# FFN down-projection: high and low parts of f 64 bytes apart, their products in turn; other activations on multiples of 256

## The chip, the cores and the metric

The kernel runs on one core of a Trainium2 chip. The metric is the device time of one execution in microseconds (us). A traced execution has a span (first to last instruction of the program) besides its time.

## The reference, cut to what matters

Two blocks for a sequence of 256 tokens of width 1024, in float32. The second half of the first block is a convolutional feed-forward network (FFN); the products in question are its last line, and every other product with a 1024-wide weight matrix shares the tiles that are moved:

```
def _conv_ffn(h, w_up, conv_w, conv_b, w_down):
    a, g = jnp.split(h @ w_up, 2, axis=-1)          # 2 x 2816 columns
    a = lax.conv_general_dilated(a, conv_w[:, None, :], window_strides=(1,), padding=[(CONV_W - 1, 0)], ...) + conv_b
    return (jax.nn.gelu(a) * g) @ w_down            # 2816 x 1024
...
    h = _rmsnorm(x, norm_g[l, 2]) * (1.0 + sc2) + sh2
    y = _conv_ffn(h, w_up[l], conv_w[l], conv_b[l], w_down[l])
    x = x + g2 * _rmsnorm(y, norm_g[l, 3])
```

Before it stands a mixer (projections of h, three small attentions, gates, an output projection); behind it a second block: a gated linear attention layer and a layer of dilated window attention, each with projections in and out and a layer norm.

## The kernel before, in words

Every float32 operand of a large product is split into a high part (rounded to float32r, "hi") and a low part (the rest, "lo"), and each product is three matmuls: lo times hi, hi times lo, hi times hi. `mm3` issues them in this order, its first operand being the stationary one (loaded by LDWEIGHTS, the profile's PEld), its second the moving one (streamed by MATMUL). In the profile's names the moving operand stands first: `acc<-whi,flo` streams whi past flo.

Weights come through `Stream`: an SP DMA fetches a chunk of 2048 columns into `raw`, ScalarE casts each half to `whi` (L158), VectorE subtracts to get `wlo` (L159). There are three raw buffers and six buffers each of whi and wlo, that is three chunks of two parts; a cast waits until TensorE is through with the buffer it writes. The chunks follow one order written out at L282 to L322; `get` casts two chunks ahead.

Two forms of product use them. `wpair` and `wstat` hold weights stationary and stream 256 tokens of an activation (output columns in partitions): the first projections, the gates, the FFN's up-projection, and the query and key projections. For these keys (`STILL`) wlo lies 64 bytes behind a multiple of 128, whi on one. `tokmm` holds 128 tokens of an activation stationary and streams 512 columns of a weight: the output projections, values, and FFN down. There wlo lies on a multiple of 128.

Activations that feed these products stand in pairs made by `big8`: tiles of 8192 bytes and 128 more in each partition, in a tag of two buffers 8320 bytes apart, so one buffer lies on a multiple of 256 and the other 128 bytes past one. hhi and h2hi (L401, L916) take the first buffer and hlo and h2lo the second; mhi and x2hi (L792, L967) the second, mlo and x2lo the first. `past` moves a tile by so many floats: h2lo by 64 bytes, x3hi by 32 and x3lo by 96. The pairs yhi/ylo (L626) and ohi/olo (L1110) are tiles of their own, all on multiples of 256.

The FFN (L952 to L962) runs over 22 row tiles f of 128 columns of the inner width. `ffn_up(f)` is one `wpair` of 48 products, then the convolution, Gelu, the multiplication and the split into `fhi` (L947, ScalarE) and `flo` (L948, VectorE), each 128 x 256 in a tag of six buffers of 1024 bytes. After every second tile one chunk of w_down is multiplied with the two tiles before: for each tile u, both blocks b of 128 tokens, both halves c of the 1024 output columns, the three products of `mm3` in a row; 24 products of 512 columns for a chunk. Two chunks are left for the end, where all four tiles are done for b=0 and then for b=1, there bank by bank. The sums lie in four PSUM banks (`acc`) for the whole loop. Behind it `rms_residual` (ORD2) and `transposes` make x2 and its transposed split x2hi/x2lo.

x2 lies in a pool `res` that stays open to the end of the kernel; pools p3 (gated linear attention) and p4 (window attention) lie behind it.

Of the kernel before, what the change touches and what calls it, by code (L numbers as in the profile page):

```python
# [9 lines left out]
F32R = mybir.dt.float32r  # L10
# [8 lines left out]
S = 256  # L19
D = 1024  # L20
KK = 8
# [177 lines left out]
def wsl(w, a, b):  # L199

    part, parts = w
    i = a // part
    assert b <= (i + 1) * part
    return tuple(t[:, a - i * part:b - i * part] for t in parts[i])
# [26 lines left out]
def hybrid_blocks(ctx, tc, A, out, dbg=None):  # L231
# [3 lines left out]
    cn = Lines(ctx.enter_context(tc.tile_pool(name="cn", bufs=1)), sm)  # L235
# [3 lines left out]
    def open_pool(name):  # L239
        st = ExitStack()  # L240
        p = st.enter_context(tc.tile_pool(name=name, bufs=1))
        return Lines(p, st.enter_context(tc.tile_pool(name=name + "s", bufs=1))), st.close
# [4 lines left out]
    def acc_t():  # L247

        return [ps.tile([128, 512], F32, tag="acc", name="acc", bufs=4) for _ in range(2)]

    def mm_t():
        return ps.tile([128, 512], F32, tag="mm", name="mm", bufs=2)
# [8 lines left out]
    def mm(o, l, r, start, stop, share=False):  # L261
        return pe.matmul(o, l, r, start=start, stop=stop, skip_group_check=share)  # L262
# [8 lines left out]
    def mm3(o, l, r, start, stop, share=False):  # L271
        mm(o, l[1], r[0], start, False, share)
        mm(o, l[0], r[1], False, False, share)
        return mm(o, l[0], r[0], False, stop, share)

    def sl(pair, *ix):
        return tuple(t[ix] for t in pair)
# [74 lines left out]
    def col(name, i):  # L352
        o = COLS[name] + i
        return cols[:, o:o + 1]
# [40 lines left out]
            mm(pr[:, 256 + b:257 + b], ssq[:, b * 128:(b + 1) * 128], ones[:, 0:1], h == 0 and b == 0, h == 3, True)  # L395

    def big8(dt, name, past=0):
        t = cn.tile([128, KK * S + 32], dt, name=name, tag="big8r", bufs=2)
        return t[:, past:past + KK * S].rearrange("p (k s) -> p k s", k=KK)

    hT = (big8(F32R, "hhi"), big8(F32R, "hlo"))  # L401
# [6 lines left out]
    def gemv(raw):  # L408

        g = p0.tile([128, 2], F32, name="gv", tag="gv", bufs=3)  # L410
        for u in range(2):
            t = p0.tile([128, D], F32, name="gj", tag="gj", bufs=1)
            ins = dve.scalar_tensor_tensor(t, raw[:, u * D:(u + 1) * D], 1.0, crow, op0=OP.mult, op1=OP.mult, accum_out=g[:, u:u + 1])
        return g, ins
# [68 lines left out]
    with tc.high_priority(400):  # L483
        ga, ins = gemv(raw)
# [8 lines left out]
    for j in range(KK):  # L493
        cur = h32
        ws.behind = at
        raw, w = ws.get(("in1", j), 1 if j + 1 < KK else None)
# [14 lines left out]
    wk = p1  # L511
# [10 lines left out]
    def wpair(key, a, fresh=False):  # L522


        w = ws.get(key)
        p = mm_t()
        if fresh:
            for n in range(2):
                o = p[:, n * 256:(n + 1) * 256]
                W = [wsl(w, n * 1024 + k * 128, n * 1024 + (k + 1) * 128) for k in range(KK)]  # L530
                for k, l in enumerate(W):
                    mm(o, l[1], a[0][:, k, :], k == 0, False)
                    mm(o, l[0], a[0][:, k, :], False, False)
                for k, l in enumerate(W):
                    mm(o, l[0], a[1][:, k, :], False, k == KK - 1)
            return p
        for n in range(2):
            wstat(p[:, n * 256:(n + 1) * 256], w, n * 1024, a)
        return p
# [199 lines left out]
    def gates(i):  # L739
        p = wpair(("zg", i), hT)  # L740
        for u in range(2):
            n, br = (i, u) if i < 8 else (2 * (i - 8) + u, 2)
            act.activation(th[:, n, min(br, 1), :], p[:, u * 256:(u + 1) * 256], AF.Tanh, scale=0.5,
                           bias=bgh[:, br * 8 + n:br * 8 + n + 1])
        next(att, None)
# [30 lines left out]
    for i in range(2):  # L776
        w = ws.get(("br", i))
        for u in range(4):
            n = 4 * i + u
# [7 lines left out]
        if i:  # L787
            w2 = ws.get(("br", 2))
            branch2(0)
            branch2(1)  # L790
        gates(9 + 2 * i)
    mT = (big8(F32R, "mhi"), big8(F32R, "mlo"))  # L792
    for i in range(4):
        if i > 1:
            branch2(i)
        merged(i)

    def tokmm(accs, work, width, first, last, bs=(0, 1), banks=(False, False)):


        for b in bs:
            steps = [(v, c) for v in enumerate(work) for c in range(0, width, 512)]
            if banks[b]:
                steps.sort(key=lambda v: v[1])
            for (i, (aT, k, w, base)), c in steps:
                l = sl(aT, slice(None), k, slice(b * 128, (b + 1) * 128))
                e = min(c + 512, width)
                ins = mm3(accs[b][c // 512][:, 0:e - c], l, wsl(w, base + c, base + e), first and i == 0, last and i == len(work) - 1)
        return ins.ins

    def tokproj(accs, keys, aT, width, tail=1, look=None, i=0):

        n = len(keys)
        while i < n:
            m = tail if i == n - tail else 1
            work = []
            for j in range(i, i + m):
                w = ws.get(keys[j], look if i == n - tail else None)
                work += [(aT, 2 * j + u, w, u * width) for u in range(2)]
            for part in ([work] if m > 1 else [work[0:1], work[1:2]]):  # L820
                ins = tokmm(accs, part, width, i == 0 and part is not work and part[0] is work[0] or (i == 0 and part is work),
                      i + m == n and part[-1] is work[-1], banks=(False, m > 1))
            i += m
        return ins
# [3 lines left out]
    last_mm = tokproj(y, [("out", i) for i in range(4)], mT, 1024, 2, 1)  # L828
# [73 lines left out]

    close_p1()
    close_p1a()
    res, _ = open_pool("res")
    ctx.callback(_)
    p2, close_p2 = open_pool("p2")
    wk = p2
    xn = p2.tile([128, 2, D], F32, name="xn")
# [22 lines left out]
    y2 = [acc_t(), acc_t()]  # L932
    fact = {}

    def ffn_up(f):
        p = wpair(("up", f), h2, f == 0)
        u = wk.tile([128, S], F32, name="u", tag="u", bufs=2)
        cw = lambda i: col("cw", i * NF + f)
        act.activation(u, p[:, 0:S], AF.Identity, scale=cw(2), bias=col("cb", f))
        dve.scalar_tensor_tensor(u[:, 1:S], p[:, 0:S - 1], cw(1), u[:, 1:S], op0=OP.mult, op1=OP.add)  # L940
        dve.scalar_tensor_tensor(u[:, 2:S], p[:, 0:S - 2], cw(0), u[:, 2:S], op0=OP.mult, op1=OP.add)
        act.activation(u, u, AF.Gelu_apprx_tanh)
        a = wk.tile([128, S], F32, name="fa", tag="fa", bufs=2)
        dve.tensor_mul(a, u, p[:, S:2 * S])
        hi = wk.tile([128, 1, S], F32R, name="fhi", tag="fhi", bufs=6)
        lo = wk.tile([128, 1, S], F32R, name="flo", tag="flo", bufs=6)
        ins = act.activation(hi[:, 0, :], a, AF.Copy)  # L947
        ins2 = dve.tensor_sub(lo[:, 0, :], a, hi[:, 0, :].bitcast(F32))  # L948
        fact[f] = (hi, lo)
        return ins, ins2  # L950

    for f in range(NF):  # L952
        ins = ffn_up(f)
        if f % 2 == 0 and 0 < f <= NF - LASTF:
            w = ws.get(("dn", f // 2 - 1))
            for u in range(2):
                tokmm(y2, [(fact[f - 2 + u], 0, w, u * 1024)], 1024, f == 2 and u == 0, False)
    work = []
    for i in range((NF - LASTF) // 2, NF // 2):
        w = ws.get(("dn", i), 1)  # L960
        work += [(fact[2 * i + u], 0, w, u * 1024) for u in range(2)]
    last_mm = tokmm(y2, work, 1024, False, True, banks=(False, True))  # L962

    x2 = res.tile([128, 2, D], F32, name="x2")
    rms_residual(y2, x1, mod[3], x2, ORD2)
# [7 lines left out]
    wk = p3  # L973
# [5 lines left out]
    w = ws.get(("gla", 8))  # L979
# [107 lines left out]
    for i in range(4):  # L1087
        w = ws.get(("gvg", i))
# [8 lines left out]
    for i in range(2):  # L1097
        w = ws.get(("gvg", 4 + i))
# [6 lines left out]
    work = []  # L1105
    for i in range(2, 4):
        w = ws.get(("gvg", 4 + i), 1)
# [5 lines left out]
    def gated(b, u, last):  # L1113

        qa, qd = Queue(tc, act, last[0]), Queue(tc, dve, last[1])
        with tc.high_priority(BOOST):
            t = sg[:, b, half(u)]
            qa.activation(t, pv[b][u], AF.Tanh, scale=0.5)
            qd.scalar_tensor_tensor(t, t, 1.0, pv[b][u], op0=OP.add, op1=OP.mult)
            qd.tensor_mul(t, t, on[:, b, half(u)])  # L1120
        return qa.last, qd.last
# [15 lines left out]
    last = ws.last  # L1137
    for u in range(2):
        last = gated(0, u, last)
    for u in range(2):  # L1140
        last = transpose_half(sg, 0, u, oT, mm_t(), last)
# [3 lines left out]
    w = ws.get(("gout", 0), 0)  # L1145
    work = [(oT, u, w, u * 1024) for u in range(2)]
    for u in range(2):
        last = gated(1, u, last)
    for u in range(2):
        tokmm(y3, work[u:u + 1], 1024, u == 0, False, (0,))  # L1150
        last = transpose_half(sg, 1, u, oT, at_t(), last)
# [3 lines left out]
    last_mm = tokproj(y3, [("gout", i) for i in range(4)], oT, 1024, 2, 1, 1)  # L1155
# [58 lines left out]
            nc.scalar.dma_start(x3d[b], x3[:, b, :])  # L1214

    close_p3()
    p4, close_p4 = open_pool("p4")
    ctx.callback(close_p4)
    wk = p4
# [89 lines left out]
    for h in range(8):  # L1309
# [8 lines left out]
        if h == 2:  # L1318
# [3 lines left out]
            for a in range(4):  # L1322
                for b in range(4):
                    q = (a % 2) * 64 + b * 16
# [7 lines left out]
        if h in (2, 6):  # L1332
            w = ws.get(("sout", h // 4))
# [4 lines left out]
    w = ws.get(("sout", 2)), ws.get(("sout", 3))  # L1338
    tokmm(y4, [(sact[4], 0, w[0], 0)], 1024, False, False)
    work = [(sact[5], 0, w[0], 1024)]  # L1340
# [103 lines left out]
```

## Time and profile before

| | |
|---|---|
| three runs | 741.21, 735.28, 741.20 us; median 741.2 |
| profiled execution: time, span | 733.62 us, 731.6 us |
| mean granted clock of the span | 0.986 |
| TensorE matmul busy | 700.6 us (96% of the span) |
| weight loads busy | 636.4 us (87%) |
| VectorE, ScalarE, GpSimd busy | 547.1, 407.1, 20.2 us |
| SP queue of the weights | 139.05 MB, 52.1% of 16 engines' span |

Matmuls overlap: a product of 256 columns is shown with some 0.28 us, one of 512 columns with 0.39 us, but the next one starts after a fraction of that. What a product costs a full TensorE is the step from its start to the next start.

### The profile page before, as it was taken

The numbers are of one execution on the slowest core, as the hardware profiler recorded it, in microseconds if no ns is written. First come the engines' busy times: TensorE is split into PE (matmuls) and PEld (weight loads), VectorE is DVE, ScalarE is ACT, GpSimd is POOL, SyncE is SP. The second block draws the span as 40 slices with busy tenths as digits, with TensorE's granted clock in tenths as the row PEclk, the third lists the DMA queues.
The fourth block names the chain that finished last, engine by engine and source line by source line (L and its number), as shares of the span: only waits on it lengthen the run. The fifth ranks groups of instructions, "written<-read, shape, count | busy, mean of one in ns | idle before, by whom it ended". The sixth has DMA issues, their size and how long they took to land. (4 is left out here: it accounts for less than half of the span.)

```text
span 731.6 us, 12192 instructions
## 1 busy us (share of the span) xinstructions
PE 700.6 (96%) x4878; PEld 636.4 (87%) x4878; DVE 547.1 (75%) x933; ACT 407.1 (56%) x675; POOL 20.2 (3%) x34
## 2 busy tenths in 40 slices
PE   4999999999979999999999899999989999999995
PEld 4888888998859999998999797888879999999984
DVE  5877969898868776768566756675777689777866
ACT  3447788546548555554545774543555556555542
POOL 0001000000010000000000200001010000000000
PEclk8999999999999999999999999999999999999999
DMA  8996768677734765758554464231437755433201
GB/s 321 418 345 237 275 257 301 229 250 255 256 136 174 276 243 178 262 207 310 201 195 174 181 224 141 109 116 58 189 142 276 261 194 168 168 125 135 89 1 57
DMA packets 24600, 148.74 MB, mean 203 GB/s; under 512 B 2992, under 2 KB 3248, under 8 KB 9568
## 3 DMA queue, kind: packets, MB, share of 16 engines
q1 hardware_dynamic: 21888, 139.05, 52.1%
q0 software_dynamic: 1280, 5.18, 2.1%
q10 hardware_dynamic: 1376, 3.74, 1.5%
q8 instruction: 38, 0.62, 0.3%
q14 instruction: 18, 0.15, 0.1%
HBM read 145.86 MB, written 2.10 MB: 202 GB/s over the span
## 5 line engine op out<-in xcount | busy, mean ns | idle before, releaser
L159 DVE TENSOR_TENSOR wlo<-raw,whi 128x1024 fp32r<-128x1024 f32 (+1 forms) x193 | 231.3, 1210 | 63.1 <-ACT whi L158 63.1
L158 ACT ACTIVATE whi<-raw 128x1024 fp32r<-128x1024 f32 (+1 forms) x193 | 199.4, 1050 | 94.1 <-PE acc L262 42.5
L262 PE MATMUL mm<-h2hi,wlo 128*128 128x256 f32 x352 | 98.3, 280 | 0.0
L262 PE MATMUL mm<-h2hi,whi 128*128 128x256 f32 x352 | 98.1, 280 | 0.0
L262 PE MATMUL mm<-h2lo,whi 128*128 128x256 f32 x352 | 97.0, 282 | 0.0
L262 PE MATMUL mm<-x3hi,wlo 128*128 128x256 f32 x304 | 86.2, 285 | 0.0
L262 PE MATMUL mm<-x3hi,whi 128*128 128x256 f32 x304 | 85.1, 281 | 0.0
L262 PE MATMUL mm<-x3lo,whi 128*128 128x256 f32 x304 | 82.9, 280 | 0.0
L262 PEld LDWEIGHTS mm<-h2hi,wlo 128*128 128x128 f32 x352 | 67.0, 190 | 0.4
L262 PEld LDWEIGHTS mm<-h2hi,whi 128*128 128x128 f32 x352 | 66.9, 190 | 0.0
L262 PEld LDWEIGHTS mm<-h2lo,whi 128*128 128x128 f32 x352 | 65.1, 188 | 0.3
L262 PE MATMUL mm<-hhi,wlo 128*128 128x256 f32 x208 | 59.5, 286 | 0.5 <-DVE wlo L159 0.3
L262 PE MATMUL mm<-hlo,whi 128*128 128x256 f32 x208 | 59.2, 285 | 0.0
L262 PE MATMUL mm<-hhi,whi 128*128 128x256 f32 x208 | 58.7, 282 | 0.0
L262 PEld LDWEIGHTS mm<-x3hi,wlo 128*128 128x128 f32 x304 | 57.7, 190 | 0.0
L262 PEld LDWEIGHTS mm<-x3hi,whi 128*128 128x128 f32 x304 | 57.5, 189 | 0.0
L262 PEld LDWEIGHTS mm<-x3lo,whi 128*128 128x128 f32 x304 | 56.2, 188 | 0.0
L262 PEld LDWEIGHTS mm<-hhi,wlo 128*128 128x128 f32 x208 | 39.0, 188 | 2.5 <-PE mm L262 0.8
L262 PEld LDWEIGHTS mm<-hlo,whi 128*128 128x128 f32 x208 | 39.1, 188 | 0.8 <-issue 0.8
L262 PEld LDWEIGHTS mm<-hhi,whi 128*128 128x128 f32 x208 | 39.1, 188 | 0.6 <-issue 0.5
L445 DVE SCALAR_TENSOR_TENSOR adacc<-raw,cact,adacc 128x1024 f32<-128x1024 f32 x28 | 35.7, 1276 | 0.2
L262 PE MATMUL acc<-whi,flo 128*128 128x512 f32 x88 | 34.8, 395 | 0.0
(355 smaller groups left out, 1604.0 us busy)
## 6 DMA issues: line engine op xcount, KB each, us to landing
raw<-in_w_up_dram SPq DMA_DIRECT2D x22, 1024.0 KB, 4.9
raw<-in_w_ada_dram SPq DMA_DIRECT2D x16, 1024.0 KB, 4.9
raw<-in_swa_q_dram SPq DMA_DIRECT2D x16, 1024.0 KB, 4.9
raw<-in_w_zg_dram SPq DMA_DIRECT2D x12, 1024.0 KB, 4.9
raw<-in_w_dn_dram SPq DMA_DIRECT2D x11, 1024.0 KB, 4.7
raw<-in_w_ada_dram SPq DMA_DIRECT2D x16, 512.0 KB, 9.0
early<-in_w_in_dram SPq DMA_DIRECT2D x8, 1024.0 KB, 7.3
raw<-in_gla_vg_dram SPq DMA_DIRECT2D x8, 1024.0 KB, 5.1
```

What stands on the lines that cost most here:

```text
L158: i0 = nc.scalar.activation(hi[:, :m], raw[:, o:o + m], AF.Copy)
L159: i1 = nc.vector.tensor_sub(lo[:, :m], raw[:, o:o + m], hi[:, :m].bitcast(F32))
L262: return pe.matmul(o, l, r, start=start, stop=stop, skip_group_check=share)
L445: dve.scalar_tensor_tensor(a, w, c, a, op0=OP.mult, op1=OP.add)
```

## The change

1. FFN down. fhi and flo get 64 floats more, and for even f flo starts 64 bytes in, for odd f fhi does. `tokmm` gets a form `turn`: the two tiles of a chunk are handed over together, each product carries the side (0 or 1) on which its stationary part lies, and `in_turn` picks, among the next 12 products of the list, the first whose side differs from the last one's. Within a tile the order is then hi times lo, lo times hi, hi times hi.
2. `big8` pads by 256 bytes in place of 128: both buffers lie on multiples of 256. hlo, mhi, x2hi lose their 128 bytes; h2lo goes from 192 to 64 modulo 256, x3lo from 224 to 96; mlo gets 64 bytes.
3. `res` is closed after p3, so p4 begins where x2 lay.

```diff
--- before.py
+++ after.py
@@ -395,7 +395,7 @@
             mm(pr[:, 256 + b:257 + b], ssq[:, b * 128:(b + 1) * 128], ones[:, 0:1], h == 0 and b == 0, h == 3, True)
 
     def big8(dt, name, past=0):
-        t = cn.tile([128, KK * S + 32], dt, name=name, tag="big8r", bufs=2)
+        t = cn.tile([128, KK * S + 64], dt, name=name, tag="big8r", bufs=2)
         return t[:, past:past + KK * S].rearrange("p (k s) -> p k s", k=KK)
 
     hT = (big8(F32R, "hhi"), big8(F32R, "hlo"))
@@ -789,24 +789,41 @@
             branch2(0)
             branch2(1)
         gates(9 + 2 * i)
-    mT = (big8(F32R, "mhi"), big8(F32R, "mlo"))
+    mT = (big8(F32R, "mhi"), big8(F32R, "mlo", 16))
     for i in range(4):
         if i > 1:
             branch2(i)
         merged(i)
 
-    def tokmm(accs, work, width, first, last, bs=(0, 1), banks=(False, False)):
+    def tokmm(accs, work, width, first, last, bs=(0, 1), banks=(False, False), turn=False):
 
 
         for b in bs:
             steps = [(v, c) for v in enumerate(work) for c in range(0, width, 512)]
             if banks[b]:
                 steps.sort(key=lambda v: v[1])
+            todo = []
             for (i, (aT, k, w, base)), c in steps:
                 l = sl(aT, slice(None), k, slice(b * 128, (b + 1) * 128))
                 e = min(c + 512, width)
-                ins = mm3(accs[b][c // 512][:, 0:e - c], l, wsl(w, base + c, base + e), first and i == 0, last and i == len(work) - 1)
+                r = wsl(w, base + c, base + e)
+                todo += [((u + i) % 2, c, l[u], r[v]) for u, v in ((0, 1), (1, 0), (0, 0)) if turn] or [
+                    (0, c, l[u], r[v]) for u, v in ((1, 0), (0, 1), (0, 0))]
+            if turn:
+                todo = in_turn(todo)
+            of = [c for _, c, _, _ in todo]
+            for n, (_, c, l, r) in enumerate(todo):
+                ins = mm(accs[b][c // 512][:, 0:min(512, width - c)], l, r, first and c not in of[:n], last and c not in of[n + 1:])
         return ins.ins
+    def in_turn(todo, ahead=12):
+        todo, done = list(todo), []
+        while todo:
+            kind = done[-1][0] if done else 1
+            done.append(todo.pop(next((n for n, v in enumerate(todo[:ahead]) if v[0] != kind), 0)))
+        return done
 
     def tokproj(accs, keys, aT, width, tail=1, look=None, i=0):
 
@@ -902,8 +919,7 @@
 
     close_p1()
     close_p1a()
-    res, _ = open_pool("res")
-    ctx.callback(_)
+    res, close_res = open_pool("res")
     p2, close_p2 = open_pool("p2")
     wk = p2
     xn = p2.tile([128, 2, D], F32, name="xn")
@@ -942,8 +958,9 @@
         act.activation(u, u, AF.Gelu_apprx_tanh)
         a = wk.tile([128, S], F32, name="fa", tag="fa", bufs=2)
         dve.tensor_mul(a, u, p[:, S:2 * S])
-        hi = wk.tile([128, 1, S], F32R, name="fhi", tag="fhi", bufs=6)
-        lo = wk.tile([128, 1, S], F32R, name="flo", tag="flo", bufs=6)
+        hi, lo = (wk.tile([128, 1, S + 64], F32R, name=n, tag=n, bufs=6) for n in ("fhi", "flo"))
+        hi, lo = (t[:, :, 16 * q:16 * q + S] for t, q in ((hi, f % 2), (lo, 1 - f % 2)))
         ins = act.activation(hi[:, 0, :], a, AF.Copy)
         ins2 = dve.tensor_sub(lo[:, 0, :], a, hi[:, 0, :].bitcast(F32))
         fact[f] = (hi, lo)
@@ -953,13 +970,12 @@
         ins = ffn_up(f)
         if f % 2 == 0 and 0 < f <= NF - LASTF:
             w = ws.get(("dn", f // 2 - 1))
-            for u in range(2):
-                tokmm(y2, [(fact[f - 2 + u], 0, w, u * 1024)], 1024, f == 2 and u == 0, False)
+            tokmm(y2, [(fact[f - 2 + u], 0, w, u * 1024) for u in range(2)], 1024, f == 2, False, turn=True)
     work = []
     for i in range((NF - LASTF) // 2, NF // 2):
         w = ws.get(("dn", i), 1)
         work += [(fact[2 * i + u], 0, w, u * 1024) for u in range(2)]
-    last_mm = tokmm(y2, work, 1024, False, True, banks=(False, True))
+    last_mm = tokmm(y2, work, 1024, False, True, banks=(False, True), turn=True)
 
     x2 = res.tile([128, 2, D], F32, name="x2")
     rms_residual(y2, x1, mod[3], x2, ORD2)
@@ -1214,6 +1230,7 @@
             nc.scalar.dma_start(x3d[b], x3[:, b, :])
 
     close_p3()
+    close_res()
     p4, close_p4 = open_pool("p4")
     ctx.callback(close_p4)
     wk = p4
```

## Rows read from the trace of the kernel before

**Rows 1.** Page, part 1, of the whole span: busy time of each engine.

```profile
PE 700.6 (96%) x4878; PEld 636.4 (87%) x4878; DVE 547.1 (75%) x933; ACT 407.1 (56%) x675; POOL 20.2 (3%) x34
```

**Rows 2.** Busy us by stretch: PE, PEld, DVE, ACT, POOL; granted clock, DMA share, GB/s.

```profile
222.00:411.00 189.00, 187.25 (x1341) 174.66 (x1341) 133.71 (x183) 101.09 (x147) 3.40 (x7) 1.00 0.59 215
...
425.00:530.00 105.00, 103.44 (x580) 88.28 (x579) 72.90 (x105) 51.68 (x79) 2.05 (x2) 1.00 0.36 132
```

**Rows 3.** What TensorE waited for, from 200 to 420 us.

```profile
PE acc L890 <- DVE xr L193: 3.1, 1, 3.1
```

**Rows 4.** Instruction groups by form, TensorE: count, busy us, mean ns.

```profile
L262 PE MATMUL mm<-h2lo,whi 128*128 128x256 f32 x352 | 97.0, 282 | 0.0
...
L262 PE MATMUL acc<-whi,flo 128*128 128x512 f32 x88 | 34.8, 395 | 0.0
```

**Rows 5.** Timeline, FFN: start us, duration us, instruction, one chunk of down, one of up.

```profile
271.60 0.40 PE L262 MATMUL acc<-whi,flo 128*128 128x512 f32 x1
...
271.60 0.19 PEld L262 LDWEIGHTS acc<-wlo,fhi 128*128 128x128 f32 x1
...
276.83 0.39 PE L262 MATMUL acc<-whi,fhi 128*128 128x512 f32 x1
...
277.06 0.28 PE L262 MATMUL mm<-h2hi,wlo 128*128 128x256 f32 x1
...
288.17 0.40 PE L262 MATMUL acc<-whi,flo 128*128 128x512 f32 x1
```

**Rows 6.** Timeline, TensorE: ends of unbroken stretches of h, y, m, x2, o, x3.

```profile
66.39 0.28 PE L262 MATMUL mm<-hhi,wlo 128*128 128x256 f32 x1
...
71.83 0.28 PE L262 MATMUL mm<-hhi,whi 128*128 128x256 f32 x1
...
144.49 0.28 PE L262 MATMUL mm<-yhi,wlo 128*128 128x256 f32 x1
...
150.15 0.28 PE L262 MATMUL mm<-hhi,wlo 128*128 128x256 f32 x1
...
191.43 0.40 PE L262 MATMUL acc<-whi,mhi 128*128 128x512 f32 x1
...
202.61 0.39 PE L262 MATMUL acc<-whi,mhi 128*128 128x512 f32 x1
...
432.55 0.28 PE L262 MATMUL mm<-x2hi,whi 128*128 128x256 f32 x1
...
438.33 0.39 PE L262 MATMUL acc<-whi,x2lo 128*128 128x512 f32 x1
...
443.88 0.39 PE L262 MATMUL at<-glamr,Ll 128*128 128x512 f32 x1
...
524.10 0.39 PE L262 MATMUL acc<-whi,olo 128*128 128x512 f32 x1
...
530.23 0.39 PE L262 MATMUL acc<-whi,olo 128*128 128x512 f32 x1
...
577.16 0.28 PE L262 MATMUL mm<-x3hi,wlo 128*128 128x256 f32 x1
...
594.14 0.38 PE L262 MATMUL at<-skT,sq 128*128 128x256 f32 x1
```

**Rows 7.** Timeline, other engines: casts, last f tile, window attention's constants.

```profile
274.54 1.06 ACT L158 ACTIVATE whi<-raw 128x1024 fp32r<-128x1024 f32 x1 [0.63 <-PE acc L262]
...
394.89 0.40 PE L262 MATMUL acc<-whi,flo 128*128 128x512 f32 x1
...
397.69 0.42 ACT L947 ACTIVATE fhi<-fa 128x256 fp32r<-128x256 f32 x1 [0.49 <-DVE fa L944]
...
398.14 0.42 DVE L948 TENSOR_TENSOR flo<-fa,fhi 128x256 fp32r<-128x256 f32 x1 [0.48 <-ACT fhi L947]
...
547.56 0.60 POOL L338 DMA_DIRECT2D ropes<-in_ropes_dram  x1 [7.01 <-DVE wlo L159]
...
550.88 0.69 DVE L550 SCALAR_TENSOR_TENSOR rope<-mm,ropes 128x512 f32<-128x512 f32 x1 [0.39 <-ACT rope L547]
```

## The prediction

> **What bounds the kernel now.** I read the busy times first: TensorE is busy for 96% of the span [rows 1]. Then the stretches: in the FFN 187.25 of 189.00 us, in the linear attention 103.44 of 105.00 us, at a granted clock of 1.00 [rows 2]. Then TensorE's waits: from 200 to 420 us they come to 6.2 us in four rows, the largest 3.1 us at transposes (L890) [rows 3], and none stands in front of a product with f. So time can come only from the step from one product to the next; a cast or a DMA that comes sooner gives nothing.
>
> Steps I read from the timeline, as the distance of two starts divided by the products between them. FFN down: 277.06 - 271.60 over 24 products, 227.5 ns. FFN up: 288.17 - 277.06 over 96, 115.7 ns [rows 5]. Elsewhere, for the same two shapes [rows 6]: h 5.44 us over 47, 115.7 ns; y 5.66 over 48, 117.9; x2 as moving operand 5.78 over 49, 118.0; m 11.18 over 48, 232.9; x2 as stationary operand 5.55 over 24, 231.3; o 6.13 over 27, 227.0; x3 as moving operand 16.98 over 144, 117.9. The mean durations of the groups can't show this: with 282 and 395 ns [rows 4] they are far longer than the steps, since products overlap.
>
> So products of one shape differ by 2% (256 columns) to 2.6% (512). With the addresses beside them: h has its high part on a multiple of 256 and takes 115.7; x2, with its high part 128 past, takes 118.0. The stationary o, with both parts on multiples of 256, takes 227.0, as f does (227.5); m and x2, with one part 128 past, take 231 to 233. And within h a weight load runs beside the product ahead of it (a load of 0.19 us starts with that product [rows 5]), so a step belongs to the pair "product streaming, weights loading". Over the starts between the first and last rows of h (16 triples): behind `hhi,wlo` 113 ns, behind `hlo,whi` 121, behind `hhi,whi` 112. The slow one is the one in which a load of whi follows a load of whi; in the others the side of the stationary part changes by 64 bytes. h2 shows it too: 114, 118 and 115 ns over 32 triples [rows 5]. But y (115, 118, 120) and x2 (117, 118, 119) do not: there changing sides gains nothing [rows 6].
>
> **The change part by part.** Products counted from the code, step changes from the rows above.
>
> 1. f, 264 products (88 of each kind [rows 4]), now all on one side, then in turn. The nearest row for 512 columns is the last product of a chunk, behind which wlo of the other side is loaded: 277.06 - 276.83 [rows 5], 226 ns in the mean of nine chunks against 227.5. I take -1.5 ns, -0.4 us. Bounds: the 256-column gain of 7.5 ns at its full size, -2.0 us; and the level of m and x2, +5.4 ns, +1.4 us. Banks change now after every third product, within those 227.5 ns, so the more frequent changes are put at nothing.
>
> 2. m, 96 products: mhi loses its 128 bytes, mlo gets 64. From 232.9 to f's 227.5: -0.5 us; bounds -0.5 and 0.
>
> 3. x2 stationary, 192 products: both parts on multiples of 256, like o. 231.3 to 227.0: -0.8 us; bounds -0.8 and 0.
>
> 4. x2 moving, 216 products (72 of each kind): 118.0 to h's 115.7: -0.5 us; bounds -0.5 and 0.
>
> 5. h, 912 products (12 x 3 x 8 at the start, 13 pairs of 48). Only hlo moves, from 128 to 0 modulo 256. Its step of 121 should fall to that of y's or h2's low part, 118: 304 x -2.7 = -0.8 us. Bounds: -0.8; and y, which lies just so already (both parts on multiples of 256) and takes 117.9: 912 x +2.2 = +2.0 us. I take the lower end, since hhi, with the two fast steps, does not move.
>
> 6. h2, 1056 products (352 of each kind [rows 4]): h2lo goes from 192 to 64. Modulo 128 nothing changes: 0. Bounds: -0.3 (low part at x2's 117.5 ns) and +2.4 us (all at x2's 118.0).
>
> 7. x3, 912 products with moving x3 (19 pairs) and some with it stationary: x3lo from 224 to 96. The same modulo 128: 0. Bounds: -2.0 (at h2's level) and 0, since no stretch of this shape is slower.
>
> 8. Waits. A chunk's second tile is wanted sooner: fhi of the odd tile by its 6th product in place of the 14th, flo by the 9th in place of the 13th. Tightest is the end: the last fhi is done at 398.11 and wanted at 394.89 + 17 x 0.2275 = 398.76, flo at 398.56 and wanted at 394.89 + 20 x 0.2275 = 399.44 [rows 7]; both are in time, by 0.65 and 0.9 us. For b=1 there the order of banks stays, so `rms_residual` starts as before. The weights' first part comes free later: after 19 of 24 products in place of 12, 7 x 0.2275 = 1.6 us. A ScalarE cast waits for that (0.63 us at 274.54 [rows 7]), with the odd tile's fhi, its activations and the next casts queued behind it on ScalarE, and the subtractions on VectorE. But the part cast at 274.54 to 275.60 is used from 288.17 on, 12.6 us later [rows 5, 7], and that fhi too is used only in the next chunk. Price 0; with that cover gone 1.6 us for each of nine chunks, 14 us.
>
> 9. `res` closed. ropes and swamask are then written over x2, whose last reader is the first step of the layer norm that makes x3; products with x3 are running when ropes is issued now (547.56 us), so it can start sooner and isn't held longer. The first reader waits 0.39 us for ScalarE, not for them [rows 7]. 0; if GpSimd issued the two ahead of that layer norm's power, at 0.60 us each, +1.2 us.
>
> Sum: -0.4 - 0.5 - 0.8 - 0.5 - 0.8 = -3.0 us. All lower bounds -6.9, all upper bounds +7.0 us. The profiled execution of 733.62 us would take 730.6. The median of the runs is 741.2, 7.6 us above it, with runs from 735.28; the shift is the same, so 738.2 us.
>
> The Trainium skill speaks against the whole of it: "TensorE: Matmul & The Clock Gate", Part 2, says that TensorE has two independent read ports, so that loading the next weights takes no bandwidth from the running matmul, and "SBUF — State Buffer", "Who interferes with whom", that TensorE never waits on anyone. By that no address matters and the sum is 0. The rows don't agree as far as they go: 112 and 121 ns stand side by side in one stretch of one shape. The first page's formula for an isolated matmul (section "Back-to-back issue gap") gives 216 ns for 512 columns; if alternation reached it, item 1 would be an estimated -3.0 us. No stretch of 512 columns comes below 227 [rows 6].
>
> **The rivals.** *Addresses are not the cause.* The differences between stages could come from what ScalarE and VectorE write meanwhile or from the weights' buffers, which follow other sequences in other stages. For it: y has the addresses that h gets and is as slow as x2; x3's two sides 64 bytes apart gain nothing. Against it: the same 112 and 121 in every triple of h. Gains and losses stay within 1 us: 741.2 us.
>
> *The multiples of 256 are the wrong place for moving operands.* y is the only pair that lies so now, and takes 117.9. If h and h2, the two fast stages, slip to that level, they cost 2.0 + 2.4 us; items 1 to 3 give back 1.7: +2.7 us, 743.9. It decides from a slip of 0.9 ns a product over their 1968 products. For it: y itself. Against: y's products come in groups of six instead of 24, and hhi and h2hi stay.
>
> *A wait takes the place.* The late release of buffers holds ScalarE's casts until products wait: up to +14 us, 752. Against it stands the slack of 12.6 us; it decides only if three or more chunks fell behind in a row.
>
> *Alternation gives its full size*, 7.5 ns on f, and x3 gains as well: -6.9 us, 734.3.
>
> **How the numbers follow.** Chances: forecast 0.55 (736 to 741), addresses no cause 0.22, slower by multiples of 256 0.12, waits 0.02, full size 0.09. The predicted time is the forecast's, 738.2. The range goes from the full size and the fast end of the runs (735.28 - 3.0 = 732.3, and 730.6 for an execution like the profiled one; I take 731) to the second rival, 744. Within 1% (7.4 us) is about what a measurement of this kernel can tell from no change: nearly all cases lie there, 0.82. Faster by over 1% takes the full size and some luck in the runs, 0.1; slower by over 1% the waits or both upper bounds, 0.08.
>
> **What would show it.** In the changed profile: 24 products of f in 5.42 us or less (226 ns) between two `ffn_up`; m and stationary x2 at 227 to 228; moving x2 at 115.7; the step behind `hlo,whi` at 118; h2 unchanged at 115.7; no new row among TensorE's waits between 238 and 406 us. The prediction is wrong if h or h2 goes to 118, if f rises above 228, or if whi casts wait for `acc` products and a product for wlo.

## The result, and the profile after

The changed kernel takes 741.06 us (median of 15 runs, 739.06 to 744.22). Before, measured beside it, takes 736.27 us (15 runs, 733.26 to 741.21; the 741.2 in the table above came from its first three). The ratio of 1.0059 (95% interval 1.0040 to 1.0079) is 4.3 us more. The forecast was 3 us less than before. One execution of the first experiment (e1), of 999.8 us at a granted clock of 0.657 where its other nine have 0.98 to 0.99, is left out of its median. The profiled execution took 741.53 us, with a span of 739.5; that of before, at 733.62, was one of its shortest, so the two traces are 7.9 us apart and not 4.3.

Part 1 of the page of the kernel after (for [rows 1]), the stretches of its FFN and linear attention with the columns of [rows 2], and TensorE's largest wait from 200 to 420 us (for [rows 3]):

```profile
PE 707.5 (96%) x4878; PEld 642.3 (87%) x4878; DVE 547.6 (74%) x933; ACT 408.6 (55%) x675; POOL 20.2 (3%) x34
```

```profile
222.00:411.00 189.00, 188.40 (x1326) 175.94 (x1327) 131.75 (x180) 102.08 (x147) 1.69 (x4) 0.99 0.60 215
425.00:530.00 105.00, 103.42 (x603) 88.82 (x602) 69.05 (x103) 54.81 (x86) 2.05 (x2) 1.00 0.35 127
```

```profile
PE acc L907 <- DVE xr L193: 3.1, 1, 3.1
```

TensorE is as full as before, has the same instructions and the same largest wait, in the transposes ahead of the FFN, and is busy 6.9 us longer (707.5 - 700.6). So the time is in the steps. The starts of its products, from the timeline, at the ends of unbroken stretches (for [rows 5 and 6]):

```profile
66.77 0.28 PE L262 MATMUL mm<-hhi,wlo 128*128 128x256 f32 x1
...
72.31 0.28 PE L262 MATMUL mm<-hhi,whi 128*128 128x256 f32 x1
...
147.92 0.28 PE L262 MATMUL mm<-yhi,wlo 128*128 128x256 f32 x1
...
153.57 0.28 PE L262 MATMUL mm<-hhi,wlo 128*128 128x256 f32 x1
...
194.78 0.40 PE L262 MATMUL acc<-whi,mhi 128*128 128x512 f32 x1
...
216.37 0.40 PE L262 MATMUL acc<-whi,mhi 128*128 128x512 f32 x1
...
241.95 0.39 PE L262 MATMUL acc<-wlo,fhi 128*128 128x512 f32 x1
...
275.74 0.39 PE L262 MATMUL acc<-wlo,fhi 128*128 128x512 f32 x1
...
281.32 0.28 PE L262 MATMUL mm<-h2hi,wlo 128*128 128x256 f32 x1
...
292.63 0.39 PE L262 MATMUL acc<-wlo,fhi 128*128 128x512 f32 x1
...
412.19 0.39 PE L262 MATMUL acc<-whi,fhi 128*128 128x512 f32 x1
...
426.75 0.28 PE L262 MATMUL mm<-x2hi,whi 128*128 128x256 f32 x1
...
445.94 0.40 PE L262 MATMUL acc<-whi,x2lo 128*128 128x512 f32 x1
...
451.21 0.39 PE L262 MATMUL acc<-whi,x2hi 128*128 128x512 f32 x1
...
584.94 0.28 PE L262 MATMUL mm<-x3hi,wlo 128*128 128x256 f32 x1
...
601.73 0.28 PE L262 MATMUL mm<-x3hi,whi 128*128 128x256 f32 x1
```

Read as the prediction read them: h (72.31 - 66.77) / 47 = 117.9 ns, from 115.7; h2 (292.63 - 281.32) / 96 = 117.8, from 115.7; f (281.32 - 275.74) / 24 = 232.5, from 227.5; y 5.65 / 48 = 117.7, m 21.59 / 93 = 232.2 and x3 16.79 / 143 = 117.4, all within 0.7 ns of before; x2 as moving operand 117.8 in the mean of the stretch, as before, as stationary operand 5.27 / 23 = 229.1, from 231.3.

The place where this can be seen without other changes is the FFN's loop, from the first product with f to the last: 412.19 - 241.95 = 170.24 us. In before it runs from 238.45 to 405.66, 167.21 us:

```profile
238.45 0.40 PE L262 MATMUL acc<-whi,flo 128*128 128x512 f32 x1
...
405.66 0.40 PE L262 MATMUL acc<-whi,fhi 128*128 128x512 f32 x1
```

Of the 4.3 us, 3.03 lie there. The clock has no part in it: in the loop the granted clock is 1.00 in before, in the change and in all eleven kernels below, and the 0.99 of the first stretch above belongs to its first 8 us, ahead of the loop and right behind the waits in the transposes (0.79 from 222 to 230 us). The rest of the span is no such measure: from the first stretch of h to the first unbroken stretch of m, before takes 125.0 us, and the kernels below 126.4 to 131.0 without regard to h's step, since small waits of the mixer differ from one execution to the next (in before 2.7 us in all, here 3.6).

### The profile page after: what moved, and what is told of

Same layout as the page of the kernel before. It is cut to its first block, busy times and chain, and to the rows that moved or that the text cites. A ratio compares the mean times of both kernels' runs of the same rounds, so it can differ in the third digit from the quotient of the medians.

```text
span 739.5 us, 12192 instructions
## 1 busy us (share of the span) xinstructions
PE 707.5 (96%) x4878; PEld 642.3 (87%) x4878; DVE 547.6 (74%) x933; ACT 408.6 (55%) x675; POOL 20.2 (3%) x34
## 5 line engine op out<-in xcount | busy, mean ns | idle before, releaser
L262 PE MATMUL mm<-hhi,whi 128*128 128x256 f32 x208 | 60.2, 289 | 0.0
L262 PEld LDWEIGHTS mm<-hhi,wlo 128*128 128x128 f32 x208 | 40.5, 195 | 3.0 <-PE mm L262 1.4
```

## The experiments

Eleven kernels, besides the change. In all of them the places of an operand are given as bytes modulo 256, high part first: in before h lies at (0, 128), h2 at (0, 192), x2 at (128, 0), m at (128, 0), x3 at (32, 224), y, o and f at (0, 0); in the change h, x2, y, o lie at (0, 0), h2 and m at (0, 64), x3 at (32, 96). One table gives the mean step of each stage, in ns, worked out from all starts in the trace of each kernel (from one start to the next where both products belong to the stage; steps more than 30% too long, which hold a wait, left out), and the FFN's loop in us as above:

```
kernel                         e1    e2      e3     e4     e5     e6     e7     e8       e9     e10    e11
stage  columns  before  after  pad   f only  sides  turn   shift  other  wlo    swapped  fast   wlo    whi
                                                           only   places one pl.         places at 192 two pl.
h      256      116.6   117.9  117.9  116.4  116.3  116.5  116.8  118.8  116.7  117.8    116.5  116.5  117.3
y      256      118.0   118.1  118.0  117.9  117.9  117.8  118.0  117.9  117.8  118.0    116.0  118.0  118.2
h2     256      115.8   117.8  117.8  116.0  115.8  115.9  115.9  118.3  119.9  116.3    115.8  115.7  118.1
x2     256      117.8   117.8  117.9  117.8  117.9  117.8  117.9  115.9  117.8  116.5    116.3  117.8  117.8
x3     256      118.0   117.9  117.9  117.9  118.0  117.9  118.0  116.5  117.9  116.6    116.5  117.6  118.2
m      512      232.0   232.2  228.2  231.9  231.8  232.0  231.8  228.3  233.5  228.4    228.2  233.4  232.3
f      512      228.1   232.3  228.5  232.4  231.5  228.0  228.0  228.4  228.3  228.0    228.0  227.7  230.0
x2     512      231.8   230.4  230.4  231.6  231.6  231.8  231.6  231.8  233.1  231.7    231.7  233.1  232.2
o      512      229.5   229.7  229.7  229.2  229.2  229.9  229.5  228.9  227.5  229.1    229.4  228.0  231.5
FFN loop, us    167.21  170.24 169.23 168.43 168.20 167.20 167.21 169.68 171.21 167.49   167.21 167.12 169.98
```

Where neither a stage's places nor its weights are touched, its mean stays within 0.5 ns for 256 columns (y 117.8 to 118.1 in nine kernels, h 116.3 to 116.8 in five) and within 1 ns for 512 (o 228.9 to 229.9 in ten); what exceeds that is a finding. The theory to be tested: the step depends on where the operands lie modulo 256, of the moving operand and of the stationary one, with nothing else of the change in it. The rivals: the new order of f's products (with its banks and its later releases); that everything behind the first buffer moved by some bytes, or `res` closed; that the stages differ by themselves and not by addresses.

**e1, the padding alone.** Of the change, `big8` at 256 bytes more and `res` closed; f as before, and mlo without its 64 bytes.

```diff
-        t = cn.tile([128, KK * S + 32], dt, name=name, tag="big8r", bufs=2)
+        t = cn.tile([128, KK * S + 64], dt, name=name, tag="big8r", bufs=2)
...
-    res, _ = open_pool("res")
-    ctx.callback(_)
+    res, close_res = open_pool("res")
...
     close_p3()
+    close_res()
```

> The kernel before with the wider padding of the activation tiles alone (and the pool of x2 closed early, which the space needs). If the multiples of 256 make h and h2 slow: h 117.8 ns a product in place of 115.7, h2 117.8 in place of 115.7, f unchanged at 227.5 to 227.8, and about 3.5 us of the 4.3 us lost, ratio 1.004 to 1.006. If the slow steps of h and h2 came with f's new order or tiles: h and h2 at 115.7 and ratio 1.000.

739.39 us (median of nine runs), ratio 1.0022 (1.0001 to 1.0043). That is less than the 1.004 to 1.006 expected. Its timeline:

```profile
195.39 0.40 PE L262 MATMUL acc<-whi,mhi 128*128 128x512 f32 x1
...
216.61 0.39 PE L262 MATMUL acc<-whi,mhi 128*128 128x512 f32 x1
...
276.33 0.39 PE L262 MATMUL acc<-whi,flo 128*128 128x512 f32 x1
...
281.81 0.28 PE L262 MATMUL mm<-h2hi,wlo 128*128 128x256 f32 x1
...
293.12 0.39 PE L262 MATMUL acc<-whi,flo 128*128 128x512 f32 x1
```

h2 takes (293.12 - 281.81) / 96 = 117.8 ns, as in the change, with f's order untouched: 5.48 / 24 = 228.3. The loop is 2.02 us longer, by 912 products of h2 x 2.0 to 2.1 = 1.9 us. And m, here at (0, 0), takes 21.22 / 93 = 228.2 ns, which the change with its 64 bytes for mlo doesn't reach. In the whole time the miss stays: h2's +2.1, h's +1.2 to 2.0, m's -0.4 and stationary x2's -0.3 us would make 2.6 to 3.4 us, and the ratio gives 1.6 (0.1 to 3.2). So h2's loss is shown here, and how much of h's reaches the time is not.

**e2, f alone.** The change with `big8` and mlo as in before (`res` closed).

```diff
-        t = cn.tile([128, KK * S + 64], dt, name=name, tag="big8r", bufs=2)
+        t = cn.tile([128, KK * S + 32], dt, name=name, tag="big8r", bufs=2)
...
-    mT = (big8(F32R, "mhi"), big8(F32R, "mlo", 16))
+    mT = (big8(F32R, "mhi"), big8(F32R, "mlo"))
```

> The kernel before with f's sides and the order in turn alone. If f's part is slow by itself: f 232.7 ns in place of 227.8, h and h2 at 115.7, about +1.2 us, ratio 1.001 to 1.002. If f's loss comes with the moved activations: f 227.8.

738.46 us (735.36 to 743.63), ratio 1.0023 (0.9999 to 1.0048). Its timeline:

```profile
274.01 0.40 PE L262 MATMUL acc<-wlo,fhi 128*128 128x512 f32 x1
...
279.59 0.28 PE L262 MATMUL mm<-h2hi,wlo 128*128 128x256 f32 x1
...
290.71 0.40 PE L262 MATMUL acc<-wlo,fhi 128*128 128x512 f32 x1
```

f takes 5.58 / 24 = 232.5 ns and h2 11.12 / 96 = 115.8. The loop is 1.22 us longer; 264 x (232.4 - 228.1) = 1.14. The two halves of the change add up: 2.02 + 1.22 = 3.24 us in the loop against 3.03 of both together.

**e3 and e4, f's places without the order, and the order without the places.** e3 is before with only the offsets of fhi and flo; e4 is e2 with all four tiles on multiples of 256.

e3, against before:

```diff
+        hi, lo = (wk.tile([128, 1, S + 64], F32R, name=n, tag=n, bufs=6) for n in ("fhi", "flo"))
+        hi, lo = (t[:, :, 16 * q:16 * q + S] for t, q in ((hi, f % 2), (lo, 1 - f % 2)))
```

e4, against e2:

```diff
-        hi, lo = (t[:, :, 16 * q:16 * q + S] for t, q in ((hi, f % 2), (lo, 1 - f % 2)))
+        hi, lo = (t[:, :, 0:S] for t, q in ((hi, f % 2), (lo, 1 - f % 2)))
```

> The kernel before with f's high and low parts on different sides, products in the order of before. If the place of the stationary part against the streamed weights sets the step (512 columns are fast when both lie alike modulo 256): f 231 to 233 ns. If it is the order in turn that costs: 227.8.

> The kernel before with the products of f in turn, all parts of f on multiples of 256. If place sets the step: f 227 to 228 ns. If the order costs (banks changing, operands changing): 231 to 233.

One run of each: e3 741.91 us, e4 737.13. The single time of e3 is no evidence: its loop takes 168.20 us, less than e2's, and the excess lies in the mixer (131.0 us from h to m). In the loop the two part cleanly. Timelines of e3 and of e4:

```profile
277.78 0.39 PE L262 MATMUL acc<-whi,flo 128*128 128x512 f32 x1
...
283.33 0.28 PE L262 MATMUL mm<-h2hi,wlo 128*128 128x256 f32 x1
```

```profile
273.73 0.40 PE L262 MATMUL acc<-wlo,fhi 128*128 128x512 f32 x1
...
279.20 0.28 PE L262 MATMUL mm<-h2hi,wlo 128*128 128x256 f32 x1
...
290.31 0.40 PE L262 MATMUL acc<-wlo,fhi 128*128 128x512 f32 x1
```

With the order in turn and all on one side, 5.47 / 24 = 227.9 ns and a loop of 167.20 us: order, banks and later releases cost nothing. With the old order and two sides, 5.55 / 24 = 231.3 ns in the chunk shown, 231.5 in the mean. The turn itself adds 0.9 ns to that (232.4). So the rival of the order falls, and alternation does not merely fail to help here: the two places cost, in either order. Whether the 64 bytes cost by themselves or only because the parts differ is open, since no run has both parts of f at 64.

**e5, everything shifted, the places kept.** e1's padding, with offsets that put each pair back where before has it modulo 256.

```diff
+    hT = (big8(F32R, "hhi", 0), big8(F32R, "hlo", 32))
...
+    mT = (big8(F32R, "mhi", 32), big8(F32R, "mlo", 0))
...
+    h2 = (big8(F32R, "h2hi", 0), big8(F32R, "h2lo", 48))
...
+    x2T = (big8(F32R, "x2hi", 32), big8(F32R, "x2lo", 0))
...
+    x3T = (big8(F32R, "x3hi", 8), big8(F32R, "x3lo", 56))
```

> The wider padding, which moves every tile behind the activations by 256 bytes, but each activation put back to its place modulo 256 of before (hlo 128, h2lo 192, mhi and x2hi 128, x3lo 224). If the place modulo 256 sets the step: h and h2 at 115.7 ns, m 232, as before. If the shift of the weights by 256 against h and h2 does it (places count modulo 512): h and h2 stay at 117.8.

737.63 us against 737.61 of before (one run each). Its timeline:

```profile
274.29 0.40 PE L262 MATMUL acc<-whi,flo 128*128 128x512 f32 x1
...
279.76 0.28 PE L262 MATMUL mm<-h2hi,wlo 128*128 128x256 f32 x1
...
290.87 0.40 PE L262 MATMUL acc<-whi,flo 128*128 128x512 f32 x1
```

f takes 5.47 / 24 = 227.9 ns and h2 11.11 / 96 = 115.7. Every stage stands within 0.3 ns of before, the loop at 167.21. The shift and `res` are out; places modulo 256 are all that counts of the padding.

**e6 and e8, other places.** Both on e1's padding. e6: h (128, 64), h2 (128, 192), x2 and x3 (0, 128), m (0, 0). e8: h (0, 64), h2 (0, 128), x2 and x3 (0, 192), m (0, 0).

e6:

```diff
+    hT = (big8(F32R, "hhi", 32), big8(F32R, "hlo", 16))
...
+    h2 = (big8(F32R, "h2hi", 32), big8(F32R, "h2lo", 48))
...
+    x2T = (big8(F32R, "x2hi", 0), big8(F32R, "x2lo", 32))
...
+    x3T = (big8(F32R, "x3hi", 0), big8(F32R, "x3lo", 32))
```

e8:

```diff
+    hT = (big8(F32R, "hhi", 0), big8(F32R, "hlo", 16))
...
+    h2 = (big8(F32R, "h2hi", 0), big8(F32R, "h2lo", 32))
...
+    x2T = (big8(F32R, "x2hi", 0), big8(F32R, "x2lo", 48))
...
+    x3T = (big8(F32R, "x3hi", 0), big8(F32R, "x3lo", 48))
```

> Other places modulo 256 (high, low): h 128, 64; h2 128, 192; x2 0, 128; x3 0, 128; m 0, 0. If a step is slow only where the streamed part and the weights loaded beside it lie alike modulo 256: h and h2, which then never do, fall to 113 to 115 ns, x3 and moving x2, now placed as h was before, to 115.7. If the high part has to lie on a multiple of 256 for the fast steps: h and h2 at 117.8, x3 and x2 at 115.7. If the stage and not the place decides: h and h2 115.7, x2 and x3 118.

> Places modulo 256 (high, low) exchanged between the stages: h 0, 64 (h2's of the changed kernel); h2 0, 128 (h's of before); x2 and x3 0, 192 (h2's of before); m 0, 0. If the places decide and not the stage: h 117.8, h2 115.7, x2 and x3 115.7 ns. If the stage decides: h and h2 as before at 115.7, x2 and x3 at 118.

One run each: 739.37 and 736.87 us (before 737.61). Timelines of e6 and of e8, h2 and x3:

```profile
282.25 0.28 PE L262 MATMUL mm<-h2hi,wlo 128*128 128x256 f32 x1
...
293.61 0.40 PE L262 MATMUL acc<-whi,flo 128*128 128x512 f32 x1
...
584.09 0.28 PE L262 MATMUL mm<-x3hi,wlo 128*128 128x256 f32 x1
...
600.61 0.28 PE L262 MATMUL mm<-x3hi,whi 128*128 128x256 f32 x1
```

```profile
281.18 0.28 PE L262 MATMUL mm<-h2hi,wlo 128*128 128x256 f32 x1
...
292.32 0.40 PE L262 MATMUL acc<-whi,flo 128*128 128x512 f32 x1
...
581.56 0.28 PE L262 MATMUL mm<-x3hi,wlo 128*128 128x256 f32 x1
...
598.09 0.28 PE L262 MATMUL mm<-x3hi,whi 128*128 128x256 f32 x1
```

h2 takes 118.3 ns in e6 and 116.0 in e8; x3, 117.9 in before, takes 16.52 / 143 = 115.5 and 16.53 / 143 = 115.6. The stage is not the cause: x2 and x3 become as fast as h was, h and h2 as slow as x3 was, at the place's bidding. Sorted by place instead of stage, over the kernels with the weights as in before, 163 of 211 unbroken stretches of 34 steps and more at (0, 128) and (0, 192) take 115.5 to 116.3 ns, and all 222 at (0, 0), (0, 64), (128, 0), (128, 64), (128, 192), (32, 96) and (32, 224) take 117.3 to 119.2. The fast places allow the fast level without securing it: of the 15 stretches with moving x3 in e9 (the table's "fast") ten take 115.5 to 116.0 ns and five 117.4 to 118.0, in e6 eight of 15 take 116.5 to 118.8, and three of h's 13 pairs in before take 118.8; hence means of 116.5. Four of e9's five are slow in e8 too, so the program decides it and not chance. All five have their weights in the same two of the six buffers, counted along the order of the chunks in the code, and two more pairs with these buffers, which run on from a product of 256 columns, are fast. In e6 the slow pairs fall on all buffers. So the place modulo 256 is not the whole condition; the weights' full address and what runs ahead of a stretch stand as rivals that no run here takes apart. What fell in e6 was my first account of it, that a step is slow only where the streamed part and the weights loaded beside it lie alike modulo 256: h and h2 lay nowhere alike there, and took 118.8 and 118.3 ns.

**e7 and e10, the places of wlo.** e7 is before with the buffers of wlo 4352 bytes apart in place of 4224, so all six lie alike (at 64 for stationary weights, at 0 for moving ones), and `res` closed. e10 puts the stationary ones at 192.

e7:

```diff
-            lo = self.pool.tile([128, 1056], F32R, tag="wlo", name="wlo", bufs=self.hlbufs)
+            lo = self.pool.tile([128, 1088], F32R, tag="wlo", name="wlo", bufs=self.hlbufs)
```

e10, besides:

```diff
-            lo = lo[:, 16:1040] if key[0] in STILL else lo[:, 0:1024]
+            lo = lo[:, 48:1072] if key[0] in STILL else lo[:, 0:1024]
```

> The kernel before with wlo's buffers 4352 bytes apart in place of 4224, so that all six lie alike modulo 256. If streamed weights of 512 columns are fast where they lie like the stationary part: o 227 in place of 229.5, the last chunks of f 227.5 in place of 229.1, s below 230, h and h2 unchanged. If the place of wlo does not count: no change.

> As the run with all buffers of wlo alike, but wlo of stationary weights 192 in place of 64 bytes past a multiple of 256. If h2 at 120 ns there came from wlo's place against h2: h2 back at 115 to 117. If it came from all buffers lying alike: h2 stays at 120.

One run each: 741.25 and 736.54 us. Timelines of e7 and of e10:

```profile
281.70 0.28 PE L262 MATMUL mm<-h2hi,wlo 128*128 128x256 f32 x1
...
293.22 0.40 PE L262 MATMUL acc<-whi,flo 128*128 128x512 f32 x1
```

```profile
280.11 0.28 PE L262 MATMUL mm<-h2hi,wlo 128*128 128x256 f32 x1
...
291.21 0.40 PE L262 MATMUL acc<-whi,flo 128*128 128x512 f32 x1
```

h2 takes 11.52 / 96 = 120.0 ns in e7, with h2 itself at (0, 192) as in before, where it was expected unchanged, and 11.10 / 96 = 115.6 in e10. So the place of the weights counts as well as that of the tokens: h2's fast place is fast for weights at 192, or at 64 and 192 in turn as in before, and not for weights at 64. For the moving wlo one place gains 1.5 to 2 ns for o (227.5 and 228.0 from 229.5) and loses 1.5 for m and stationary x2, whose high parts lie at 128.

**e11, whi at two places.** Before, with the buffers of whi 4224 bytes apart, at 0 and 128 in turn (`res` closed).

```diff
-            hi = self.pool.tile([128, 1024], F32R, tag="whi", name="whi", bufs=self.hlbufs)
+            hi = self.pool.tile([128, 1056], F32R, tag="whi", name="whi", bufs=self.hlbufs)
```

> The kernel before with whi's buffers 4224 bytes apart in place of 4096, so that every second one lies 128 bytes past a multiple of 256. If the place of the streamed part against the weights decides: h turns slow (118) and x2 fast (115.7) in the halves of a chunk whose whi lies 128 past, so both come to 116.5 to 117 in the mean. If the activation's own address decides: h 115.7 to 116.6 and x2 117.8 throughout.

739.94 us, one run; a loop of 169.98 us. Timeline:

```profile
275.08 0.39 PE L262 MATMUL acc<-whi,flo 128*128 128x512 f32 x1
...
280.60 0.28 PE L262 MATMUL mm<-h2hi,wlo 128*128 128x256 f32 x1
...
291.94 0.39 PE L262 MATMUL acc<-whi,flo 128*128 128x512 f32 x1
```

f takes 5.52 / 24 = 230.0 ns, h2 118.1. Half of the products keep whi at 0. In h, behind `hhi,whi`, `hhi,wlo` and `hlo,whi`, those with whi at 0 stay near their steps of before (115.6, 115.7 and 119.1 ns, from 114.4, 115.2 and 120.1) and those at 128 lose them (118.1, 117.0 and 118.9, from 114.3, 114.6 and 120.7): what counts for h is the place of tokens against weights. But x2, with its high part at 128, does not become fast where whi lies at 128 too (116.8, 117.3 and 119.2). So it is not the difference of two addresses alone, and this test stays half decided.

**e9, the fast places everywhere.** On e1's padding: h (0, 128), h2 (0, 192), x2 (0, 128), x3 (0, 192), m (0, 0), ylo moved to 128 for y (0, 128); f and its order as in before.

```diff
+    hT = (big8(F32R, "hhi", 0), big8(F32R, "hlo", 32))
...
-    yT = (p1.tile([128, 6, S], F32R, name="yhi", tag="yhi"), p1.tile([128, 6, S], F32R, name="ylo", tag="ylo"))
+    yT = (p1.tile([128, 6, S], F32R, name="yhi", tag="yhi"), p1.tile([128, 6 * S + 64], F32R, name="ylo", tag="ylo")[:, 32:32 + 6 * S].rearrange("p (k s) -> p k s", k=6))
...
+    mT = (big8(F32R, "mhi", 0), big8(F32R, "mlo", 0))
...
+    h2 = (big8(F32R, "h2hi", 0), big8(F32R, "h2lo", 48))
...
+    x2T = (big8(F32R, "x2hi", 0), big8(F32R, "x2lo", 32))
...
+    x3T = (big8(F32R, "x3hi", 0), big8(F32R, "x3lo", 48))
```

> Each pair at the fastest place seen for its form: f, m and their order as before on multiples of 256, moving pairs with the high part on a multiple of 256 and the low part 128 or 192 past one (h, x2, y 128; h2, x3 192). If places decide in every stage: y and x2 115.7 to 116.5 ns in place of 118, x3 116.6, m 228.3, h and h2 as before; some 2.5 us less than before, ratio 0.997. If the gains of single stages are lost again in others: ratio 1.000.

733.02 us (median of 12 runs, 731.61 to 739.22) against 736.90 of before (17 runs): ratio 0.9968 (0.9941 to 0.9995), 2.4 us less than before (0.4 to 4.3 by the interval). Timeline:

```profile
148.83 0.28 PE L262 MATMUL mm<-yhi,wlo 128*128 128x256 f32 x1
...
154.27 0.28 PE L262 MATMUL mm<-yhi,whi 128*128 128x256 f32 x1
...
582.08 0.28 PE L262 MATMUL mm<-x3hi,wlo 128*128 128x256 f32 x1
...
598.62 0.28 PE L262 MATMUL mm<-x3hi,whi 128*128 128x256 f32 x1
```

y takes 5.44 / 47 = 115.7 ns and x3 16.54 / 143 = 115.7. By the table, x3 gains 912 x 1.5, m 96 x 3.8, x2 216 x 1.5 and y 144 x 2.0 ns, in sum 2.3 us, beside the 2.4 of the ratio.

## Why the prediction was wrong

The reading that bounds the kernel held: only steps count, they depend on addresses, and no wait appeared. "Addresses are not the cause" fell with e1, e5 and e8. What failed is where I placed three terms between their bounds. The forecast's sum was -3.0 us; the measured terms below come to 4.1 to 4.9 us, beside the 4.3 of the kernel's time. That the measured 741.06 us still lies inside the stated range of 731 to 744, 2.9 us from the forecast of 738.2, is luck: the 741.2 it started from was 4.9 us above the median of 15 runs, and that error made up for most of the wrong shift.

- **Item 1, f: predicted -1.5 ns, measured +4.2 (232.3 from 228.1), 264 products, +1.1 us.** The price was the last product of a chunk, one step of 226 ns, which I took for the effect of a load from the other side. The upper bound, the level of m and x2 (+5.4 ns), was nearer: what these have in common with the new f is a part that does not lie on a multiple of 256. e4 and e3 show it: one side 228.1 and 228.0 in either order, two sides 231.5 and 232.4. The last step itself goes with f's place and not with the load behind it: in the mean of nine chunks it takes 225.8 ns in e4 and 232.4 in the change. What alternation does in h at 256 columns was carried over to 512 columns, where no kind of step in the changed chunks shows it (means of 230.5 to 234.0 ns by the two products it joins).
- **Item 6, h2: predicted 0, measured +2.0 ns, 1056 products, +2.1 us.** This is the largest term, and rested on "modulo 128 nothing changes". From 192 to 64 is nothing modulo 128, and it cost the whole difference between the fast and the slow level; e1 shows it alone. The bounds held the value (+2.4 us).
- **Item 5, h: predicted -0.8 us, measured +1.3 to +2.2 ns (mean of all steps, unbroken stretches), 912 products, +1.2 to 2.0 us.** y was named as the row with the same addresses, at 117.9 ns; I took the lower end "since hhi, with the two fast steps, does not move". The step belongs to the pair, as the prediction itself had said, so the high part's products changed with the low part's place: behind `hhi,whi` 119.1 ns in the stretch shown, from 112.3. The 115.7 it started from was a fast stretch besides: all of h in before averages 116.6. Its share of the time can't be told from one execution, beside the mixer's waits.
- **Item 2, m: predicted -0.5 us, measured 0.** f's level was the right price for (0, 0): e1 has 228.2. The change moves mlo to 64, and with any part off a multiple of 256, stationary m, f and x2 took 231 ns or more in every run here. The change says so in its second item; I priced only the loss of 128 bytes.
- **Item 3, stationary x2: predicted -4.3 ns, measured -1.4 (231.8 to 230.4), 192 products, -0.3 us.** Right in sign, a third of the size.
- **Item 4, moving x2: predicted -2.3 ns, measured 0.** The level of h was that of (0, 128). At (0, 0) x2 takes what y takes there.
- **Items 7 to 9 were right:** x3 118.0 and 117.9 ns, and the constants loaded into x2's place hold nothing up (ropes is issued at 554.28 us and first read at 558.46, behind ScalarE). The weights are held longer, as worked out, without a wait: the cast that waits for `acc` in the chunk shown starts 4.61 us after the chunk, from 2.94 [rows 5 and 7], 1.7 us later where 1.6 was forecast, and TensorE has no wait at all in the loop.

Casts of a chunk and the end of the loop in after, from the timeline (for [rows 7]):

```profile
280.35 2.24 ACT L158 ACTIVATE whi<-raw 128x1024 fp32r<-128x1024 f32 x2 [0.86 <-PE acc L262]
...
404.54 0.42 DVE L965 TENSOR_TENSOR flo<-fa,fhi 128x256 fp32r<-128x256 f32 x1 [0.48 <-ACT fhi L964]
...
405.94 0.39 PE L262 MATMUL acc<-whi,flo 128*128 128x512 f32 x1
```

The last flo is done at 404.96, and its first product, the 21st of the block that began at 401.30, starts at 405.94; the last fhi is done at 404.51 and wanted by the 18th, at 405.24. Both slacks of item 8 held, at 0.98 and 0.73 us.

The second rival, that multiples of 256 are the wrong place for moving operands, had the right outcome for h and h2, both at y's level, and its shift of +2.7 us is the nearest to the 4.3. It was sized at +2.7 us because items 1 to 3 were to give 1.7 back; they took 0.8 net (+1.1, 0, -0.3). Its wording is too wide, however: (0, 0) is wrong for a moving operand, but e9 has every high part on a multiple of 256 and is fast. And h2's slow place is (0, 64).

The Trainium skill ("SBUF — State Buffer", "Who interferes with whom") says that TensorE never waits on anyone. The prediction drew from it that no address matters and the sum is 0, which was nearer to the time than the forecast. The sentence speaks of other engines and holds in the loop, where nothing is waited for; the reading does not agree with the runs: places alone move the step from 115.7 to 117.8 ns in e1, and to 120.0 in e7.

## What to carry to other kernels

Where TensorE is full, the place of both operands is a term of 1 to 4% of its step (115.7 against 117.8 and 120.0 ns, 228 against 232), and the two roles want different places: here a stationary operand wants both parts on multiples of 256 bytes, a moving one its high part on a multiple of 256 and its low part 128 or 192 past one (the same distance from 128 or 32 on was slow, in x2 and x3 of before); a tile used in both roles, as x2 is, has to choose by its product counts. When such a term is forecast, take the row that has exactly the new pair of addresses (y for h), or the nearest such row (m for f), over one that explains the old steps, and compare levels, not single steps. Measure it in a stretch of the program that repeats to 0.01 us between kernels that leave its places alone, as the FFN's loop does here, rather than by the kernel's time.

## What the runs showed of the hardware beyond that

- By addresses alone, stretches of the same products lie on distinct levels: h2 at 115.7 ns in before, 117.8 in the change and in e1, 118.3 in e6 and 120.0 in e7; f at 227.5 and 232.5.
- In before, e4, e5 and e9, four kernels that share the loop's places and differ elsewhere, the FFN's loop of 264 + 912 products takes 167.20 or 167.21 us: whatever of ScalarE, VectorE and the DMA beside it differs from one execution to the next does not scatter it.
- Not settled: why these places. In h and h2 of before and in h, h2 and x2 of after, the step behind a product goes with the place of the part streamed before it against the weights it uses: means of 118.4 to 121.1 ns where both lie alike modulo 256, 114.4 to 116.0 otherwise. But x3, which lies nowhere alike and takes 118.0, x2 of before (117.5 otherwise), e6's h at (128, 64), e7's h2 and e11's x2 don't follow that, and at 512 columns it is the other way round in the stages' means (228 to 230.4 ns with both stationary parts on multiples of 256, like the streamed whi, and 231 to 234 otherwise). What makes five stretches of e9's x3 slow, and whether the load or the stream is held back, was not tried by itself.
